# Delta-rule layer: diagonal blocks solved on 128 partitions, moved by copies and 32x32 transposes; the inverses placed earlier in the layer's order

## The chip, the cores and the metric

The kernel runs on one core of a Trainium2 chip. The metric is device time in microseconds (us), the median of several executions. Engines: TensorE (PE, with its weight loads PEld), VectorE (DVE), ScalarE (ACT), GpSimd (POOL), and SyncE (SP), which issues the weight DMAs. Each engine runs its own instructions in the order in which they stand; they wait for each other by semaphores.

## The reference

A decoder trunk of four residual layers over 256 tokens of width 1024: pooling mixer, gated delta rule, latent attention, pooling mixer. The change touches the second. Its core, for each of 8 heads and each chunk of tokens:

```python
L = jnp.where(strict, jnp.einsum('bhnid,bhnjd->bhnij', k_beta, k) * decay, 0.0)
A = jnp.eye(C, dtype=L.dtype) + L
rhs = jnp.concatenate([v_beta, k_beta * jnp.exp(g)[..., None]], axis=-1)
sol = lax.linalg.triangular_solve(A, rhs, left_side=True, lower=True)
...
def step(state, xs):
    q_c, k_c, u_c, w_c, g_c, a_c = xs
    v_new = u_c - jnp.einsum('bhck,bhkv->bhcv', w_c, state)
    o = (jnp.einsum('bhck,bhkv->bhcv', q_c * jnp.exp(g_c)[..., None], state)
         + jnp.einsum('bhij,bhjv->bhiv', a_c, v_new))
    ...
```

So a unit lower triangular matrix I + L has to be inverted for each head and chunk.

## The kernel before, in words

Every large product goes through `project`: 512 columns of a weight matrix are loaded by SP in units of two slices of 128 rows (`weights`, L133), each slice is split into a high part on ACT (L149, `whi`) and a low part on DVE, for a few slices on POOL (L150, `wlo`), and PE accumulates three products of split operands (L162). The raw loads have three buffers, the split slices a ring of them, so PE can lag behind the splits. A projection "by channels" (`chan`) has matmuls of 256 columns, one by rows has 512.

The delta-rule layer (`gdn_layer`) takes two tiles of 128 tokens (`NT` = 2) and eight heads, in place of chunks of 64. The string `order` fixes the sequence in which its parts are written: `g` gates, `k` keys (projection, convolution on DVE L750, SiLU on ACT L787, transposes L793), `d` decays, `a` the lower triangles `LT` (L806 on PE, L813 on DVE), `s` the substitution, `q` queries, `v` values (a value's convolution L750, SiLU L902, transposes L906, scaling into `vR` L909), `V` and `c` the two halves of the last value, `i` the inverses, `u` the new values of the first tile. A scheduler then interleaves the written instructions on each engine; its result is fixed when the program is built.

The substitution inverts the 32x32 diagonal blocks of I + L, 64 of them (2 tiles x 8 heads x 4 blocks). Eight DMAs gather them from `LT` into DRAM (`d_l`, L838) and one loads them as `Lb`, one block on each of 64 partitions (L841). Then POOL runs 31 steps of a multiply (L846, into `pr`) and a subtraction (L850, in `Tb`). Step r updates the n = 31 - r rows below row r in c = r + 1 columns, n x c elements on each partition. `Tb` goes back through DRAM (`d_t`, L853, L857) into the diagonal blocks of `T`.

The inverses transpose `T` into `U` by 32x32 blocks on DVE (L929), join blocks in pairs (L938, L940, L944, L947) and then whole (L952, L953, L956, L959, L962, L965), tile after tile; the instructions of PE alternate with DVE or ACT in each. `U` is needed by the new values (L979) and by the recurrence that ends the layer, which begins with L1006 on PE.

Tiles named by `big` share one pool of buffers: a new tile waits until the last reader of its buffer's former tile is done. Before the change the second `kqT` of the queries has the buffer of `Lb`.

Of the kernel before, what the change touches and what calls it, by code (L numbers as in the profile page):

```python
# [8 lines left out]
F32 = mybir.dt.float32  # L9
# [7 lines left out]
P = 128  # L17
D = 1024
S = 256
NT = S // P  # L20
# [22 lines left out]
def trunk(ctx: ExitStack, tc: tile.TileContext, x, positions, norm_g, pool_w_in, pool_w_grp,  # L43
          pool_scale, pool_w_out, gdn_w_in, gdn_conv, gdn_a_log, gdn_dt_bias, gdn_norm_g,
          gdn_w_out, mla_w_in, mla_q_norm_g, mla_w_uq, mla_kv_norm_g, mla_w_ukv, mla_w_out,
          final_g, out, depth=4, final=True):
    nc = tc.nc
# [4 lines left out]
    const = ctx.enter_context(tc.tile_pool(name="const", bufs=1))  # L52
# [11 lines left out]
    dram = ctx.enter_context(tc.tile_pool(name="dram", bufs=1, space=bass.MemoryType.DRAM))  # L64


    def big(name, *dims, dt=F32):
        return s4.tile([P, *dims], dt, tag="s4", name=name)
# [4 lines left out]
    def workb(name, *dims):  # L73
        return wb.tile([P, *dims], F32, tag="wb", name=name)

    def small(name, *dims, bufs=2):
        return sm.tile([P, *dims], F32, tag=name, name=name, bufs=bufs)

    def bank(pool, name):
        return pool.tile([P, CW], F32, tag=name, name=name)  # L80
# [29 lines left out]
    def inorder(a, n=P):  # L110

        if len(a.shape) == 3 and a.shape[2] != n:
            a = a.rearrange("p h s -> p (h s)")
        if len(a.shape) == 3:
            return a.rearrange("p h (a b) -> p h a b", b=2)
        return a.rearrange("p (g a b) -> p g a b", a=n // 2, b=2)

    def woven(a, n=P):

        if len(a.shape) == 3 and a.shape[2] != n:  # L120
            a = a.rearrange("p h s -> p (h s)")
        if len(a.shape) == 3:
            return a.rearrange("p h (b a) -> p h a b", b=2)
        return a.rearrange("p (g b a) -> p g a b", a=n // 2, b=2)
# [191 lines left out]
    half = const.tile([P, 1], F32, name="half")  # L316
# [291 lines left out]
    GC = {}  # L608

    def gdn_setup():  # L610
        w_in = gdn_w_in[0]
        utri = const.tile([P, P], F32, name="utri")
        nc.gpsimd.memset(utri, 1.0)
        nc.gpsimd.affine_select(out=utri, in_=utri, compare_op=ALU.is_ge, fill=0.0, base=0,
                                pattern=[[1, P]], channel_multiplier=-1)
        maskT = const.tile([P, P], F32, name="maskT")
        nc.gpsimd.memset(maskT, 0.0)
        nc.gpsimd.affine_select(out=maskT, in_=maskT, compare_op=ALU.is_ge, fill=NEG, base=0,
                                pattern=[[1, 2], [2, P // 2]], channel_multiplier=-1)
        m32 = const.tile([P, 2, 32], F32, name="m32")  # L620
        nc.gpsimd.memset(m32, 0.0)
        for a in range(2):
            nc.gpsimd.memset(m32[64 * a + 32:64 * a + 64, a], 1.0)
        half = const.tile([P, NT, GDN_H // 2], F32, name="halves")
        nc.gpsimd.memset(half, -0.5)


        crow = workb("crow", P)
        nc.scalar.dma_start(out=crow, in_=gdn_conv[0].rearrange("k (n p) -> (k n) p", p=P))
        tap = const.tile([P, P], F32, name="tap")  # L630
        ps = bank(tps, "tp")
        nc.tensor.transpose(ps[:, :P], crow, ident)
        nc.vector.tensor_copy(tap, ps[:, :P])

        bw = workb("bw", KD, 16)
        bws = const.tile([P, KD, 2, 16], F32R, name="bws")
        nc.scalar.dma_start(out=bw, in_=w_in[:, 2 * GDN_QK + 2 * GDN_V:].rearrange(
            "(k p) c -> p k c", p=P))
        nc.vector.tensor_copy(bws[:, :, 0, :], bw)
        nc.vector.tensor_tensor(out=bws[:, :, 1, :], in0=bw, in1=bws.bitcast(F32)[:, :, 0, :],  # L640
                                op=ALU.subtract)
        alog = const.tile([P, GDN_H], F32, name="alog")
        nc.scalar.dma_start(out=alog, in_=gdn_a_log[0:1, :].to_broadcast([P, GDN_H]))
        dtb = const.tile([P, GDN_H], F32, name="dtb")
        nc.scalar.dma_start(out=dtb, in_=gdn_dt_bias[0:1, :].to_broadcast([P, GDN_H]))
        GC.update(utri=utri, maskT=maskT, m32=m32, half=half, tap=tap, bws=bws,
                  alog=alog, dtb=dtb)

    def gdn_layer(i, j, hT):
        H = GDN_H  # L650
        M = NT * H
        DV = 256
        w_in = gdn_w_in[j]
        utri, maskT, m32, half, tap, bws, alog, dtb = (
            GC[n] for n in ("utri", "maskT", "m32", "half", "tap", "bws", "alog", "dtb"))

        def sc(name):
            return small(name, NT, H, bufs=1)
# [11 lines left out]
                gated = nc.scalar.activation(*unpaired(gs[vi][:, t, :], banks[t]), AF.Silu)  # L670
            mark["gate"] = gated.ins

        order = "g0 k0 d a0 g1 k1 a1 s q0 v0 v1 v2 q1 V3 i c3 g2 u0 u1 g3".split()
        while order[0][0] == "g":
            gate(int(order.pop(0)[1]))

# [9 lines left out]
        for t in range(NT):  # L686
# [8 lines left out]
                                in1=dtb[:, None, :].to_broadcast([P, NT, H]))  # L695
# [13 lines left out]
                                in1=alog[:, None, :].to_broadcast([P, NT, H]))  # L709
# [14 lines left out]
        for t in range(NT):  # L724
            nc.gpsimd.dma_start(
                out=Gb[t].rearrange("p h s -> p (h s)"),
                in_=d_g[t * H:(t + 1) * H, :].rearrange("(a h) s -> a (h s)", a=1).to_broadcast(
                    [P, H * P]))
# [24 lines left out]


        Q, B = 4, 32
        Tb = big("Tb", B, B)[:M * Q]
        nc.gpsimd.memset(Tb, 0.0)
        nc.gpsimd.memset(Tb.rearrange("m r c -> m (r c)")[:, ::B + 1], 1.0)
        Ts = big("T", NT, H, P)
        T = [Ts[:, t] for t in range(NT)]  # L760
        for t in range(NT):
# [39 lines left out]
        def against(dst, rhs, sf, hf, t):  # L801

            ps = bank(aux, "aux").rearrange("p (b s) -> p b s", b=4)
            tt = slice(t * P, (t + 1) * P)
            for b in range(4):
                nc.tensor.matmul(ps[:, b], lhsT=kT[hf][:, b, tt], rhs=rhs[hf][:, b, tt],  # L806
                                 start=True, stop=True)
            for b in range(4):
                h = 4 * hf + b
                o, v, d = dst[t][:, h, :], ps[:, b], DT[t][:, h, :]  # L810
                if dst is LT:
                    o, v, d = inorder(o), inorder(v), woven(d)
                nc.vector.scalar_tensor_tensor(  # L813
                    out=o, in0=v, scalar=sf[:, t, h:h + 1], in1=d, op0=ALU.mult, op1=ALU.mult)

        LT = [big("LT", H, P) for _ in range(NT)]
# [11 lines left out]
        def lower(hf):  # L828
            for t in range(NT):
                against(LT, kT, s2, hf, t)  # L830

        def substitution():

            d_l = dram.tile([M * Q, B * B], F32, name="d_l")
            lv = d_l.rearrange("(t m d) (r c) -> t d r m c", t=NT, d=Q, r=B)
            for t in range(NT):
                for d in range(Q):
                    nc.sync.dma_start(out=lv[t, d],  # L838
                                      in_=LT[t][d * B:(d + 1) * B, :, d * B:(d + 1) * B])
            Lb = big("Lb", B, B)[:M * Q]  # L840
            nc.sync.dma_start(out=Lb, in_=d_l.rearrange("m (r c) -> m r c", r=B))  # L841
            pr = small("pr", 256, bufs=1)[:M * Q]
            for r in range(B - 1):
                n, c = B - 1 - r, r + 1
                pv = pr[:, :n * c].rearrange("m (a b) -> m a b", a=n)
                nc.gpsimd.tensor_tensor(out=pv, op=ALU.mult,  # L846
                                        in0=Lb[:, r, r + 1:, None].to_broadcast([M * Q, n, c]),
                                        in1=Tb[:, r:r + 1, :c].to_broadcast([M * Q, n, c]))
                tv = Tb[:, r + 1:, :c]
                mark["blocks"] = nc.gpsimd.tensor_tensor(out=tv, in0=tv, in1=pv,  # L850
                                                         op=ALU.subtract).ins
            d_t = dram.tile([M * Q, B * B], F32, name="d_t")
            nc.gpsimd.dma_start(out=d_t.rearrange("m (r c) -> m r c", r=B), in_=Tb)  # L853
            tv = d_t.rearrange("(m d) (r c) -> d r m c", d=Q, r=B)
            for d in range(Q):
                dd = slice(d * B, (d + 1) * B)
                nc.gpsimd.dma_start(out=Ts[dd, :, :, dd].rearrange("p t h c -> p (t h) c"),  # L857
                                    in_=tv[d])
            nc.vector.reciprocal(rki, rk)
            nc.vector.tensor_tensor(out=kds, in0=rk[:, 0, :], in1=DT[0][:, :, P - 1],  # L860
                                    op=ALU.mult)
            nc.vector.tensor_scalar(neG, eG[:, 1, :], -1.0, None, ALU.mult)
            nc.gpsimd.tensor_tensor(out=ktok, in0=ktok, op=ALU.mult,
                                    in1=kds[:, :, None].to_broadcast([P, H, P]))
# [52 lines left out]
        u1 = []  # L917
# [84 lines left out]
        st, vn, v2 = {}, {}, {}  # L1002
# [408 lines left out]
```

## Time and profile before

| | before |
|---|---|
| median of 3 runs | 829.0 us (827.01 to 829.16) |
| profiled execution: time, span | 832.1 us, 830.4 us |
| granted TensorE clock, mean | 0.986 |
| busy, share of the span: PE, DVE, ACT, POOL | 96%, 73%, 59%, 19% |
| delta-rule layer, first gate to the recurrence's first product | about 175 to 355 us |

PE's matmuls overlap in a pipeline, so its busy share alone doesn't tell whether it waits; the slices, the granted clock and the list of waits do. In rows of waits the numbers are the total, the count and the longest. In rows of instructions, start and duration come first; in brackets is how long the engine was idle before and what ended that. The lines themselves stand in the prediction.

### The profile page before, as it was taken

The numbers are of one execution on the slowest core, as the hardware profiler recorded it, in microseconds if no ns is written. First come the engines' busy times: TensorE is split into PE (matmuls) and PEld (weight loads), VectorE is DVE, ScalarE is ACT, GpSimd is POOL, SyncE is SP. The second block draws the span as 40 slices with busy tenths as digits, with TensorE's granted clock in tenths as the row PEclk, the third lists the DMA queues.
The fourth block names the chain that finished last, engine by engine and source line by source line (L and its number), as shares of the span: only waits on it lengthen the run. The fifth ranks groups of instructions, "written<-read, shape, count | busy, mean of one in ns | idle before, by whom it ended". The sixth has DMA issues, their size and how long they took to land.

```text
span 830.4 us, 16162 instructions
## 1 busy us (share of the span) xinstructions
PE 799.4 (96%) x5966; PEld 758.0 (91%) x5966; DVE 603.4 (73%) x1141; ACT 492.9 (59%) x993; POOL 159.8 (19%) x296
## 2 busy tenths in 40 slices
PE   8989999999898979999999999999999999999996
PEld 7989988989898978788989999999999989999996
DVE  4699887666987967356666678778877767877772
ACT  6665565567855655255566564666665565566662
POOL 2001100334236992023121112000000120000012
PEclk9999999999999989899999999999999999999998
DMA  6865666756655544303647786653552547576662
GB/s 204 224 180 167 193 209 210 221 153 195 193 135 180 163 139 118 124 12 115 187 125 224 231 180 185 192 164 102 153 175 80 179 143 214 183 223 202 202 204 51
DMA packets 109079, 139.90 MB, mean 168 GB/s; under 512 B 21316, under 2 KB 51208, under 8 KB 109000
## 3 DMA queue, kind: packets, MB, share of 16 engines
q1 hardware_dynamic: 106608, 137.12, 55.0%
q0 software_dynamic: 528, 1.58, 0.6%
q8 instruction: 47, 0.77, 0.4%
q10 hardware_dynamic: 1864, 0.17, 0.2%
q14 instruction: 32, 0.26, 0.1%
HBM read 137.27 MB, written 1.58 MB: 167 GB/s over the span
## 4 chain that ended last, share of the span: by engine, by line
PE 67%; DVE 11%; POOL 8%; DMA 8%; issue 4%; ACT 2%; SPq 0%; POOLq 0%; DVEq 0%; ACTq 0%
PE acc L162 53%; PE aux L162 7%; POOL pr L846 3%; DVE wlo L154 3%; POOL Tb L850 2%; DMA raw<-in_pool_w_out_dram 2%; DVE wlo L150 1%; DMA raw<-in_pool_w_in_dram 1%; DVE win L551 1%; DMA T<-d_t 1%; DMA Lb<-d_l 1%; DVE h L397 1%; DMA Gb<-d_g 1%; PE aux L979 1%; PE tp L1314 1%
## 5 line engine op out<-in xcount | busy, mean ns | idle before, releaser
L150 DVE TENSOR_TENSOR wlo<-raw,whi 128x512 fp32r<-128x512 f32 (+1 forms) x366 | 254.2, 719 | 104.3 <-ACT whi L149 100.8
L149 ACT CAST whi<-raw 128x512 fp32r<-128x512 f32 (+1 forms) x380 | 223.7, 617 | 167.6 <-PE acc L162 82.3
L162 PE MATMUL acc<-hTh,whi 128*128 128x256 f32 x832 | 230.7, 278 | 2.3 <-ACT gsg L670 1.5
L162 PE MATMUL acc<-hTl,whi 128*128 128x256 f32 x832 | 231.2, 278 | 0.0
L162 PE MATMUL acc<-hTh,wlo 128*128 128x256 f32 x832 | 229.8, 277 | 0.0
L162 PEld LDWEIGHTS acc<-hTh,whi 128*128 128x128 f32 x832 | 160.7, 193 | 2.9 <-ACT gsg L670 1.7
L162 PEld LDWEIGHTS acc<-hTl,whi 128*128 128x128 f32 x832 | 160.8, 193 | 0.3
L162 PEld LDWEIGHTS acc<-hTh,wlo 128*128 128x128 f32 x832 | 160.7, 193 | 0.1
L162 PE MATMUL acc<-wlo,yTh 128*128 128x256 f32 (+1 forms) x384 | 112.7, 312 | 0.8 <-DVE wlo L154 0.8
L162 PE MATMUL acc<-whi,yTh 128*128 128x256 f32 (+1 forms) x384 | 112.3, 315 | 0.0
L162 PE MATMUL acc<-whi,yTl 128*128 128x256 f32 (+1 forms) x384 | 89.1, 313 | 0.0
L162 PEld LDWEIGHTS acc<-wlo,yTh 128*128 128x128 f32 x384 | 73.2, 191 | 4.8 <-DVE wlo L154 1.7
L162 PEld LDWEIGHTS acc<-whi,yTh 128*128 128x128 f32 x384 | 72.9, 191 | 3.1
L162 PEld LDWEIGHTS acc<-whi,yTl 128*128 128x128 f32 x384 | 63.1, 191 | 3.4
L154 DVE SCALAR_TENSOR_TENSOR wlo<-raw,colsT,whi 128x512 fp32r<-128x512 f32 x64 | 47.0, 769 | 21.1 <-ACT whi L153 20.7
L153 ACT ACTIVATE whi<-raw,gain 128x512 fp32r<-128x512 f32 x64 | 43.6, 720 | 31.1 <-DMA raw<-in_pool_w_in_dram 22.6
L153 ACT ACTIVATE whi<-raw,colsT 128x512 fp32r<-128x512 f32 x64 | 43.5, 720 | 30.9 <-DMA raw<-in_pool_w_out_dram 18.0
L385 POOL TENSOR_TENSOR hg<-x,gain 128x256 f32<-128x256 f32 x16 | 13.4, 850 | 244.1 <-DVE x L450 244.1
L162 PE MATMUL acc<-wlo,hTh 128*128 128x512 f32 (+1 forms) x144 | 54.8, 385 | 1.9 <-DVE wlo L150 1.3
L154 DVE SCALAR_TENSOR_TENSOR wlo<-raw,gain,whi 128x512 fp32r<-128x512 f32 x64 | 46.6, 748 | 11.1 <-ACT whi L153 11.1
L162 PE MATMUL acc<-whi,hTh 128*128 128x512 f32 (+1 forms) x144 | 52.7, 379 | 0.7 <-ACT hTh L242 0.7
L162 PE MATMUL acc<-whi,hTl 128*128 128x512 f32 (+1 forms) x144 | 42.5, 373 | 0.0
(364 smaller groups left out, 1530.9 us busy)
## 6 DMA issues: line engine op xcount, KB each, us to landing
raw<-in_pool_w_in_dram SPq DMA_DIRECT2D x62, 512.0 KB, 4.4
raw<-in_gdn_w_in_dram SPq DMA_DIRECT2D x48, 512.0 KB, 4.0
raw<-in_pool_w_out_dram SPq DMA_DIRECT2D x32, 512.0 KB, 4.4
raw<-in_mla_w_in_dram SPq DMA_DIRECT2D x24, 512.0 KB, 4.5
raw<-in_mla_w_uq_dram SPq DMA_DIRECT2D x36, 256.0 KB, 3.4
raw<-in_pool_w_grp_dram SPq DMA_DIRECT2D x16, 512.0 KB, 3.8
raw<-in_gdn_w_out_dram SPq DMA_DIRECT2D x16, 512.0 KB, 3.8
raw<-in_mla_w_ukv_dram SPq DMA_DIRECT2D x32, 256.0 KB, 3.3
```

The source lines that it names most:

```text
L149: a = nc.scalar.copy(hi, v)
L150: b = e.tensor_tensor(out=lo, in0=v, in1=hi.bitcast(F32), op=ALU.subtract)
L153: a = nc.scalar.activation(hi, v, AF.Copy, scale=g)
L154: b = e.scalar_tensor_tensor(out=lo, in0=v, scalar=g, in1=hi.bitcast(F32), op0=ALU.mult, op1=ALU.subtract)
L162: return nc.tensor.matmul(inorder(o, n), lhsT=lhs, rhs=woven(rhs, n), start=start, stop=stop)
L385: nc.gpsimd.tensor_tensor(out=self.early[t, a], in0=xs[t][:, sl], in1=self.g[:, sl], op=ALU.mult)
L397: nc.vector.scalar_tensor_tensor(out=h[:, cut:], in0=xs[t][:, sl], scalar=r[:, 0:1], in1=self.g[:, sl], op0=ALU.mult, op1=ALU.mult)
L551: nc.vector.tensor_tensor(out=nxt[:, :, d:], in0=cur[:, :, d:], in1=cur[:, :, :S - d], op=ALU.add)
L846: nc.gpsimd.tensor_tensor(out=pv, op=ALU.mult, in0=Lb[:, r, r + 1:, None].to_broadcast([M * Q, n, c]), in1=Tb[:, r:r + 1, :c].to_broadcast ...
L850: mark["blocks"] = nc.gpsimd.tensor_tensor(out=tv, in0=tv, in1=pv, op=ALU.subtract).ins
L979: nc.tensor.matmul(ps[:, c], lhsT=U[0][:, h, :], rhs=vR[h // 2][:, 0, c * DV:(c + 1) * DV], start=True, stop=True)
L1314: nc.tensor.transpose(ps[:, a * P:(a + 1) * P], sb[:, a * P:(a + 1) * P], ident)
```

## The change

The 64 blocks are spread over all 128 partitions: partition p of a 32-partition band holds for one of the 16 tile-and-head pairs either the even or the odd columns of the block, 16 of 32. Each step then has c = r // 2 + 1 columns. The blocks reach `Lb` by copies into `Lg` (tile 0 on POOL, tile 1 on ACT) and one DVE transpose of 32x32 blocks that reads each block twice; the result goes back by a second such transpose into the other half of `solve` and four copies into `T`, two on POOL and two on ACT. All DMAs of this part fall away. `which`, built in layer 0, marks the even and the odd half and gives the unit diagonal. In `order` the inverses `i` move from behind `V3` to behind `v1`.

```diff
+        cols = workb("cols", 2, 32)
+        for a in range(2):
+            nc.gpsimd.memset(cols[:, a, :16], 1.0 - a)
+            nc.gpsimd.memset(cols[:, a, 16:], float(a))
+        which = const.tile([P, 2, 32], F32, name="which")
+        nc.vector.transpose(which.rearrange("p a c -> p (a c)"), cols.rearrange("p a c -> p (a c)"))
...
-        order = "g0 k0 d a0 g1 k1 a1 s q0 v0 v1 v2 q1 V3 i c3 g2 u0 u1 g3".split()
+        order = "g0 k0 d a0 g1 k1 a1 s q0 v0 v1 i v2 q1 V3 c3 g2 u0 u1 g3".split()
...
-        Tb = big("Tb", B, B)[:M * Q]
+        C = B // 2
+        solve = big("solve", 2, B, C)
+        Tb, turned_ = solve[:, 0], solve[:, 1]
         nc.gpsimd.memset(Tb, 0.0)
-        nc.gpsimd.memset(Tb.rearrange("m r c -> m (r c)")[:, ::B + 1], 1.0)
+        for a in range(2):
+            nc.gpsimd.tensor_copy(Tb.rearrange("p r c -> p (r c)")[:, a * C::B + 1],
+                                  which[:, a, :C])
+        Lg = small("Lg", M, B, bufs=1)
...
         def lower(hf):
             for t in range(NT):
                 against(LT, kT, s2, hf, t)
+                hs = slice(4 * hf, 4 * hf + 4)
+                for d in range(Q):
+                    dd = slice(d * B, (d + 1) * B)
+                    o = Lg[dd, t * H + 4 * hf:t * H + 4 * hf + 4]
+                    if t:
+                        nc.scalar.copy(o, LT[t][dd, hs, dd])
+                    else:
+                        nc.gpsimd.tensor_copy(o, LT[t][dd, hs, dd])
...
-            d_l = dram.tile([M * Q, B * B], F32, name="d_l")
-            lv = d_l.rearrange("(t m d) (r c) -> t d r m c", t=NT, d=Q, r=B)
-            for t in range(NT):
-                for d in range(Q):
-                    nc.sync.dma_start(out=lv[t, d],
-                                      in_=LT[t][d * B:(d + 1) * B, :, d * B:(d + 1) * B])
-            Lb = big("Lb", B, B)[:M * Q]
-            nc.sync.dma_start(out=Lb, in_=d_l.rearrange("m (r c) -> m r c", r=B))
-            pr = small("pr", 256, bufs=1)[:M * Q]
+            Lb = big("Lb", B, B)
+            nc.vector.transpose(Lb, Lg.rearrange("p m c -> p c m")[:, :, None, :].to_broadcast(
+                [P, B, 2, M]))
+            pr = small("pr", 136, bufs=1)
             for r in range(B - 1):
-                n, c = B - 1 - r, r + 1
+                n, c = B - 1 - r, r // 2 + 1
                 pv = pr[:, :n * c].rearrange("m (a b) -> m a b", a=n)
                 nc.gpsimd.tensor_tensor(out=pv, op=ALU.mult,
-                                        in0=Lb[:, r, r + 1:, None].to_broadcast([M * Q, n, c]),
-                                        in1=Tb[:, r:r + 1, :c].to_broadcast([M * Q, n, c]))
+                                        in0=Lb[:, r + 1:, r:r + 1].to_broadcast([P, n, c]),
+                                        in1=Tb[:, r:r + 1, :c].to_broadcast([P, n, c]))
...
-            d_t = dram.tile([M * Q, B * B], F32, name="d_t")
-            nc.gpsimd.dma_start(out=d_t.rearrange("m (r c) -> m r c", r=B), in_=Tb)
-            tv = d_t.rearrange("(m d) (r c) -> d r m c", d=Q, r=B)
+            nc.vector.transpose(turned_.rearrange("p r c -> p (r c)"),
+                                Tb.rearrange("p r c -> p c r"))
+            tv = turned_.rearrange("p r c -> p (r c)").rearrange("p (c m) -> p m c", m=M)
             for d in range(Q):
                 dd = slice(d * B, (d + 1) * B)
-                nc.gpsimd.dma_start(out=Ts[dd, :, :, dd].rearrange("p t h c -> p (t h) c"),
-                                    in_=tv[d])
+                o = Ts[dd, :, :, dd].rearrange("p t h c -> p (t h) c")
+                if d % 2:
+                    nc.scalar.copy(o, tv[dd])
+                else:
+                    nc.gpsimd.tensor_copy(o, tv[dd])
```

The change adds lines ahead of most of the layer, so line numbers move: L750 becomes L756, L793 L804, L806 L817, L906 L923, L909 L926, L929 L946, L979 L996, L1006 L1023. Outside this layer the engines' orders are the same but for the setup's five small instructions and one matmul of layer 0.

DVE, in the stretch in which v2 is convolved (`vc`) while the next weight slices are split. Before:

```order
L750 SCALAR_TENSOR_TENSOR vc<-acc,tap,vc 128x254
L750 SCALAR_TENSOR_TENSOR vc<-acc,tap,vc 128x253
L750 SCALAR_TENSOR_TENSOR vc<-acc,tap,vc 128x255
L150 TENSOR_TENSOR wlo<-raw,whi 128x512
L750 SCALAR_TENSOR_TENSOR vc<-acc,tap,vc 128x253
L750 SCALAR_TENSOR_TENSOR vc<-acc,tap,vc 128x255
L150 TENSOR_TENSOR wlo<-raw,whi 128x512
L750 SCALAR_TENSOR_TENSOR vc<-acc,tap,vc 128x254 x2
L150 TENSOR_TENSOR wlo<-raw,whi 128x512
L750 SCALAR_TENSOR_TENSOR vc<-acc,tap,vc 128x253 x2
L150 TENSOR_TENSOR wlo<-raw,whi 128x512 x3
```

And now:

```order
L756 SCALAR_TENSOR_TENSOR vc<-acc,tap,vc 128x255
L866 STREAM_TRANSPOSE solve<-solve 128x512
L150 TENSOR_TENSOR wlo<-raw,whi 128x512
L756 SCALAR_TENSOR_TENSOR vc<-acc,tap,vc 128x253
L756 SCALAR_TENSOR_TENSOR vc<-acc,tap,vc 128x255
L150 TENSOR_TENSOR wlo<-raw,whi 128x512
L756 SCALAR_TENSOR_TENSOR vc<-acc,tap,vc 128x254 x2
L756 SCALAR_TENSOR_TENSOR vc<-acc,tap,vc 128x253
L150 TENSOR_TENSOR wlo<-raw,whi 128x512
L756 SCALAR_TENSOR_TENSOR vc<-acc,tap,vc 128x253
L150 TENSOR_TENSOR wlo<-raw,whi 128x512 x2
L946 STREAM_TRANSPOSE U<-T 128x1024 x2
```

The transpose of the solved blocks (L866) now stands in the middle of v2's convolution, and the transposes into `U` directly behind it; before, they stood behind the second queries.

ACT, where v1 is scaled into `vR`. Before:

```order
L902 ACTIVATE vc<-vc 128x512
L149 CAST whi<-raw 128x512 x2
L909 ACTIVATE vR<-tp,rki 128x256 x4
L149 CAST whi<-raw 128x512 x3
L902 ACTIVATE vc<-vc 128x512 x2
```

And now:

```order
L919 ACTIVATE vc<-vc 128x512
L149 CAST whi<-raw 128x512 x2
L926 ACTIVATE vR<-tp,rki 128x256 x2
L873 COPY T<-solve 32x16x32 x2
L926 ACTIVATE vR<-tp,rki 128x256 x2
L149 CAST whi<-raw 128x512 x3
L919 ACTIVATE vc<-vc 128x512 x2
```

Two of the copies into `T` stand between the scalings; this `vR` now has the buffer of `Lb`, and the second `kqT` of the queries has one of its own.

PE, at the end of the inverses and the start of the recurrence. Before, the second tile's last steps follow each other:

```order
L162 MATMUL acc<-whi,hTl_2253 128x512 x2
L962 MATMUL aux<-U,X 64x64 x8
L952 MATMUL aux<-ident,U 64x64 x8
L956 MATMUL aux<-T,LT 128x64 x8
L962 MATMUL aux<-U,X 64x64 x8
L979 MATMUL aux<-vR,U 128x256 x8
L1006 MATMUL aux<-u_4405,ktok 128x256 x2
```

And now the first of the new values come behind the last step of the second tile, with accumulations of the last gate (`hTh`, `hTl` are the layer's input) between them:

```order
L162 MATMUL acc<-whi,hTh_2250 128x512
L979 MATMUL aux<-U,X 64x64 x8
L817 MATMUL aux<-kqT 128x128 x8
L996 MATMUL aux<-vR,U 128x256 x2
L162 MATMUL acc<-wlo,hTh_2250 128x512
L162 MATMUL acc<-whi,hTl_2251 128x512 x2
L162 MATMUL acc<-whi,hTh_2250 128x512
L162 MATMUL acc<-wlo,hTh_2250 128x512
L162 MATMUL acc<-whi,hTh_2250 128x512
```

In all, 30 accumulations stand between the last L996 and the recurrence's L1023, where there were none; ahead of the last L979 stand 17 behind its L973, 22 and 26 between the steps before.

More of the change, by code (lines that the diff above doesn't have):

```diff
@@ L645, in gdn_setup @@
         nc.scalar.dma_start(out=dtb, in_=gdn_dt_bias[0:1, :].to_broadcast([P, GDN_H]))
-        GC.update(utri=utri, maskT=maskT, m32=m32, half=half, tap=tap, bws=bws,
+        GC.update(utri=utri, maskT=maskT, m32=m32, half=half, which=which, tap=tap, bws=bws,
                   alog=alog, dtb=dtb)
@@ L653, in gdn_layer @@
         w_in = gdn_w_in[j]
-        utri, maskT, m32, half, tap, bws, alog, dtb = (
-            GC[n] for n in ("utri", "maskT", "m32", "half", "tap", "bws", "alog", "dtb"))
+        utri, maskT, m32, half, which, tap, bws, alog, dtb = (
+            GC[n] for n in ("utri", "maskT", "m32", "half", "which", "tap", "bws", "alog", "dtb"))
         def sc(name):
```

## The prediction

> **What bounds the kernel now.** I read the chain of work that ended last first, then the busy time and the granted TensorE clock in slices of 4 us, then who waits for whom, then the instructions of the engines named there.
>
> ```profile
> PE 67%; DVE 11%; POOL 8%; DMA 8%; issue 4%; ACT 2%; SPq 0%; POOLq 0%; DVEq 0%; ACTq 0%
> ```
>
> Two thirds of the chain are matmuls, so an edit pays only where TensorE (PE) stands still or runs at a lower clock. POOL, busy for 19% of the span, holds 8% of the chain: nearly all of it is the substitution (L846, L850) between 255 and 301 us, with the DMAs ahead of it and behind it. The slices below carry window, length, then for PE, PEld, DVE, ACT and POOL busy us and instructions, then clock, DMA share, GB/s.
>
> ```profile
> 268.00:272.00 4.00, 2.02 (x17) 1.83 (x16) 4.00 (x9) 2.39 (x4) 3.69 (x5) 0.96 0.53 139
> 272.00:276.00 4.00, 4.00 (x25) 4.00 (x24) 4.00 (x9) 3.27 (x8) 3.61 (x6) 0.62 0.66 203
> ...
> 296.00:300.00 4.00, 0.14 (x2) 0.00 (x0) 1.11 (x3) 0.00 (x0) 3.38 (x9) 0.87 0.43 136
> 300.00:304.00 4.00, 3.17 (x15) 3.17 (x16) 2.68 (x5) 3.22 (x7) 3.70 (x8) 0.50 0.07 16
> 304.00:308.00 4.00, 4.00 (x30) 4.00 (x30) 2.33 (x4) 1.40 (x3) 4.00 (x5) 0.78 0.32 53
> ...
> 344.00:348.00 4.00, 2.55 (x23) 2.27 (x21) 1.79 (x3) 0.58 (x1) 0.00 (x0) 0.84 0.38 133
> 348.00:352.00 4.00, 4.00 (x21) 3.43 (x20) 0.68 (x1) 0.41 (x2) 0.00 (x0) 0.50 0.01 4
> 352.00:356.00 4.00, 4.00 (x15) 3.07 (x14) 0.33 (x1) 2.84 (x8) 0.00 (x0) 0.80 0.00 0
> ```
>
> Three holes show, each followed by slices at a lower clock. What PE waited for in them (us in total, times, longest):
>
> ```profile
> PE tp L793 <- ACT kqT L787: 4.7, 1, 4.7
> PE tp L906 <- ACT vc L902: 2.5, 2, 2.0
> PE acc L162 <- DVE vc L750: 0.8, 1, 0.8
> PE aux L962 <- DVE X L959: 0.8, 1, 0.8
> PE aux L956 <- ACT T L953: 0.7, 1, 0.7
> ...
> ACT kqT L787 <- POOL pr L846: 5.5, 1, 5.5
> ```
>
> **Hole A**, 269 us: the transposes of v0 wait 2.0 us for its convolution on VectorE (DVE), which is busy for all of the slices 268 to 276. The lower clock costs 0.04x4 + 0.38x4 = 1.7 us: 3.7 us together.
> **Hole B**, 296 us: ScalarE (ACT) can't write the second q until POOL's last multiply, because that kqT gets the buffer of Lb. PE loses 4.7 us, and 0.50x4 + 0.22x4 = 2.9 us of clock behind it: 7.6 us.
> **Hole C**, 344 to 356 us: the last steps of the inverses stand alone on PE and wait for DVE and ACT (0.8 + 0.7 us); clock 0.16x4 + 0.50x4 + 0.20x4 = 3.4 us: 4.9 us.
> Beside these stands a wait of 0.8 us for v2's convolution at 288 us, where V3 needs an accumulator.
>
> **The substitution, shorter and sooner.**
>
> ```profile
> L846 POOL TENSOR_TENSOR pr<-Lb,Tb 64x31 f32<-64x31 f32 (+15 forms) x31 | 21.3, 686 | 16.9 <-DMA Lb<-d_l 14.5
> L850 POOL TENSOR_TENSOR Tb<-Tb,pr 64x31 f32<-64x31 f32 (+15 forms) x31 | 19.2, 620 | 2.4
> L150 DVE TENSOR_TENSOR wlo<-raw,whi 128x512 fp32r<-128x512 f32 x24 | 21.3, 898 | 2.9 <-ACT whi L149 2.9
> ...
> 255.39 0.23 POOL L846 TENSOR_TENSOR pr<-Lb,Tb 64x31 f32<-64x31 f32 x1 [14.55 <-DMA Lb<-d_l]
> 255.70 0.26 POOL L850 TENSOR_TENSOR Tb<-Tb,pr 64x31 f32<-64x31 f32 x1
> ...
> 275.86 0.62 POOL L846 TENSOR_TENSOR pr<-Lb,Tb 64x255 f32<-64x255 f32 x1
> ```
>
> It runs from 255.4 to 300.6 us: 45.2, of which 40.5 busy and 4.7 gaps. The rows of 31 and 255 elements give (0.62 - 0.23)/224 = 1.74 ns an element and 0.18 us fixed. So 62 x 0.18 = 11.2 us are fixed, and the multiplies' and subtractions' 5,456 elements each (the sum of n x c in the loop) take about 20.1; the rest, some 9 us, is blocking: the DVE subtraction of two SBUF operands, L150, takes 898 ns in the mean here and 0.69 us alone (the row at 257.11 below), and 9/24 = 0.37 us of POOL's time goes to each of the 24. In the change c is r//2 + 1, which sums to 2,856 elements, 52%. That gives 11.2 + 4.7 + 0.52 x 20.1 + 18 blockings of 0.37 (18 such DVE instructions now stand beside it) = 33 us. The bounds: 26 us without any blocking, and 45 us, as long as now, should an instruction on 128 partitions cost twice what it does on 64. I take 33: POOL's multiply of 128x512 below takes 1.27 us, which fits 0.18 + 512 x 1.74 = 1.07 and some blocking, and not twice that.
>
> Its start: LT is done at 242.82 + 1.89 = 244.7 us, and Lb is there 10.6 us later, through eight DMAs and one back.
>
> ```profile
> 242.82 1.89 DVE L813 SCALAR_TENSOR_TENSOR LT<-aux,s,DT 128x128 f32<-128x128 f32 x7
> 243.70 3.79 SPq L838 DMA_DIRECT2D d_l<-LT  x8
> 249.16 0.45 SPq L841 DMA_DIRECT2D Lb<-d_l  x1
> ...
> 256.46 0.62 ACT L149 CAST whi<-raw 128x512 fp32r<-128x512 f32 x1 [2.92 <-DMA raw<-in_gdn_w_in_dram]
> 257.11 0.69 DVE L150 TENSOR_TENSOR wlo<-raw,whi 128x512 fp32r<-128x512 f32 x1 [2.85 <-ACT whi L149]
> ...
> 314.95 2.37 DVE L929 STREAM_TRANSPOSE U<-T 128x1024 f32<-128x1024 f32 x2 [3.06 <-DMA T<-d_t]
> ```
>
> Now four copies on POOL and four on ACT take that place, side by side, 128 elements each: between 0.23 us (31 elements on POOL) and 0.62 (255 on POOL, 512 on ACT); I take 0.3, nearer to the first, and both engines are done at 246. The DVE transpose of 128x1024 takes 2.37/2 = 1.2 us and stands behind queued work, near 248. The solve starts at 249.5 and ends at 282.5 us.
>
> SP's nine issues go as well, with the weight loads held behind them: DVE's idle 2.85 us at 254 (a whi that waited 2.92 us for its load) goes, and DVE runs 2.9 us ahead through the convolutions. That closes hole A: **-3.7 us**. The new 1.2 us transpose falls into the other idle time of DVE in this stretch.
>
> **What now waits for the solve.** DVE's transpose of the result (L866) stands between the convolutions of v2, ACT's copies into T (L873) and v1's vR, which now gets Lb's buffer, between the scalings of v1.
>
> ```profile
> 283.47 1.25 DVE L750 SCALAR_TENSOR_TENSOR vc<-acc,tap,vc 128x254 f32<-128x254 f32 x3
> 284.64 0.68 DVE L150 TENSOR_TENSOR wlo<-raw,whi 128x512 fp32r<-128x512 f32 x1
> ...
> 300.60 1.27 POOL L878 TENSOR_TENSOR Gb<-Gb,kqT 128x512 f32<-128x512 f32 x1
> 303.48 1.85 POOL L772 TENSOR_TENSOR rq<-rq,halves 128x8 f32<-128x8 f32 x1
> ```
>
> L866 stands between these two DVE rows, at 284.6 less 2.9 and less some blocking: near 281. So DVE and ACT wait some 1.5 us for the solve's end at 282.5; behind DVE are queued weight subtractions and the rest of v2's convolution, which V3's accumulator waits for. Half of an 128x1024 transpose is 0.6 us, then the 4.8 us of queue that stand there now: v2 is done at 288. PE, 3.7 us earlier by hole A, is there at 288.3 - 3.7 = 284.6 and waits 3.5 us in place of 0.8: **+2.7**. A wait of that size cost 1.7 us of clock in hole A: **+1.7**.
> T: POOL first does L895 and a power (1.27 and 1.85 us as above) with two small instructions, then its two copies of 512 elements (0.62 to 1.27 each, I take 0.8): T is whole near 289, DVE's U transposes are due at 291, and PE gets to the first pairs at 289 to 290. DVE is the later one, so this costs little.
> Hole B goes, since no buffer of q waits for Lb any more: **-7.6**. Hole C goes: by the order the last steps of both tiles now have 15 to 30 accumulations between them, as only the first tile's had before:
>
> ```profile
> 332.62 4.95 PE acc L162 x22
> ```
>
> Twenty-two of them cover 4.95 us, and DVE and ACT answer in one: **-4.9**. In their place I count 1.5 us of short waits (PE for the masked X behind the U transposes, and for an accumulator under the second q's scores): **+1.5**. ACT's first four copies of LT stand ahead of the second keys' convolution: 4 x 0.3 = **+1.2**; the other four stand ahead of weight casts, which are prefetched, and cost nothing unless that lead is used up (then 1.2 more). The setup's four memsets and one small transpose lie beside layer 0's matmuls, at nothing; without that cover they cost five short instructions, 5 x 0.23 = 1.2 us.
>
> **Sum**: -3.7 + 2.7 + 1.7 - 7.6 - 4.9 + 1.5 + 1.2 = **-9.1 us**. Against the profiled execution's 832.1 us (830.4 of span and 1.7 around it) that is 823.0. The median of the runs is 829.0, 3.1 below that execution, so I predict 829.0 - 9.1 = **819.9 us**.
>
> [...] The two first POOL rows have 31 elements each, but the second reads and writes a column of Tb, 128 bytes from element to element: 0.26 against 0.23 us, 1 ns an element. The new multiply reads a column of Lb in the same way. [...]
>
> **Rivals.**
> 1. Column reads lengthen the solve: 2,856 x 1 ns = 2.9 us by the rows above, passed on whole through L866: -9.1 + 2.9 = -6.2, 822.8 us. For it: the pair of rows. Against: rows of longer runs show no such difference, and runs grow to 16. Chance 0.17.
> 2. The tail keeps its waits: in-order DVE and ACT put X, U and T behind convolutions and weight work, and hole C moves rather than goes: -9.1 + 4.9 = -4.2, 824.8 us. Chance 0.13.
> 3. The solve ends before DVE gets to L866 (blocking nearly gone, 30 us or less): L866's 1.5 us, the clock's 1.7 and the 1.5 of short waits fall away: -9.1 - 4.7 = -13.8, 815.2 us. Chance 0.1.
> 4. The other side: an instruction on 128 partitions costs twice its element time, the solve takes 45 us and ends at 294.7. DVE, ACT and then PE stand still at L866 12.2 us longer, with 1.2 us more of clock (hole B's 2.9 against 1.7): -9.1 + 13.4 = +4.3, 833.3 us. It decides from a solve of some 42 us on. Chance 0.06.
> 5. The change does not free PE: the wait for Lb only passes from q to v1's vR and L866, with a solve near 40 us: -9.1 + 7 = -2.1, 826.9 us. Chance 0.04.
>
> **How the numbers follow.** The forecast has 0.5. A measurement of this kernel can tell about 0.3%, 2.5 us, from no change. Cases 1 to 3 and the forecast are faster by more: 0.9; case 5 is the same, 0.04; case 4 slower, 0.06. The range goes from just under case 3, 814.5, to past case 2, 826; the solve's upper bound, case 4, stays outside with case 5.
>
> **What would show it.** Right: no wait of kqT for POOL; a solve of about 33 us that starts near 249.5; L866 waiting 1 to 3 us; one PE wait of 3 to 4 us near 285; full clock from 340 on; the recurrence's first product (L1006, now L1023) near 346 instead of 355 us. Wrong: a solve over 40 us, a wait of DVE at L866 over 5 us, or PE waits of more than 3 us in all between 290 and 345.

## The result, and the profile after

| | before | after |
|---|---|---|
| median, first comparison (6 runs each) | 829.08 us (827.01 to 830.99) | 823.74 us (819.74 to 824.35) |
| ratio to before | | 0.9928, 95% interval 0.9904 to 0.9952 |
| measured again (11 and 6 runs) | 830.19 us | 825.98 us, ratio 0.9949, 0.9929 to 0.9969 |
| profiled execution: time, span | 832.1 us, 830.4 us | 824.35 us, 822.6 us |

The forecast was 819.9 us, with a range of 814.5 to 826.0. The change is faster, as forecast, but brings 4 to 5 us, not 9. The two profiled executions lie 7.8 us apart. Part of that lies ahead of the edited stretch, as the rows of the first convolution and of the recurrence's first product show (durations in ns, then first and last start):

```profile
L750 DVE SCALAR_TENSOR_TENSOR cv<-acc,tap,cv x48: 460/474/483, 197.5 to 304.2; 128x255 f32<-128x255 f32 x16, 128x254 f32<-128x254 f32 x16, 128x253 f32<-128x253 f32 x16
L1006 PE MATMUL aux<-u,ktok x16: 379/379/382, 355.0 to 372.8; 128*128 128x256 f32 x16
```

Before, the recurrence begins 355.0 - 197.5 = 157.5 us behind the first convolution. After:

```profile
L756 DVE SCALAR_TENSOR_TENSOR cv<-acc,tap,cv x48: 460/472/483, 196.0 to 304.1; 128x255 f32<-128x255 f32 x16, 128x254 f32<-128x254 f32 x16, 128x253 f32<-128x253 f32 x16
L1023 PE MATMUL aux<-u,ktok x16: 379/379/382, 346.6 to 365.0; 128*128 128x256 f32 x16
```

346.6 - 196.0 = 150.6 us, 6.9 less. I call this distance the stretch; it compares profiles without what happens ahead of it. The slices of the changed kernel (window, length, then PE, PEld, DVE, ACT, POOL busy, clock, DMA share, GB/s):

```profile
268.00:272.00 4.00, 4.00 (x37) 4.00 (x38) 4.00 (x9) 3.42 (x9) 3.61 (x6) 1.00 0.61 200
...
280.00:284.00 4.00, 2.62 (x24) 2.42 (x22) 0.00 (x0) 0.21 (x1) 3.14 (x12) 1.00 0.00 0
284.00:288.00 4.00, 0.00 (x0) 0.00 (x0) 3.91 (x8) 3.43 (x6) 3.86 (x6) 0.91 0.00 0
288.00:292.00 4.00, 3.33 (x15) 3.07 (x15) 3.69 (x6) 4.00 (x10) 3.49 (x5) 0.50 0.52 138
292.00:296.00 4.00, 4.00 (x21) 4.00 (x20) 4.00 (x7) 1.61 (x4) 0.00 (x0) 0.50 0.58 145
296.00:300.00 4.00, 4.00 (x32) 4.00 (x32) 3.05 (x7) 2.90 (x7) 0.00 (x0) 0.81 0.33 117
...
340.00:344.00 4.00, 4.00 (x20) 3.52 (x19) 1.29 (x2) 2.08 (x5) 0.00 (x0) 1.00 0.18 62
```

Holes A, B and C are gone (no slice from 300 to 360 us is below full clock), and one new hole stands at 283 us, with a low clock from 287 to 297 us. Who waited for whom there, on PE, DVE and ACT:

```profile
PE acc L162 <- DVE vc L756: 5.9, 1, 5.9
...
DVE solve L866 <- POOL solve L864: 6.6, 1, 6.6
...
ACT vR L926 <- POOL pr L860: 7.0, 1, 7.0
```

PE waits for v2's convolution, which is queued behind L866 on DVE, which waits for the solve. ACT stands for the same time at v1's vR, whose buffer was Lb's. The rows around it (start, duration, idle before):

```profile
249.29 0.61 POOL L860 TENSOR_TENSOR pr<-Lb,solve 128x31 f32<-128x31 f32 x1 [5.03 <-DVE Lb L854]
...
283.83 0.22 POOL L864 TENSOR_TENSOR solve<-solve,pr 128x16 f32<-128x16 f32 x1
...
276.23 1.25 DVE L756 SCALAR_TENSOR_TENSOR vc<-acc,tap,vc 128x254 f32<-128x254 f32 x3
284.09 1.05 DVE L866 STREAM_TRANSPOSE solve<-solve 128x512 f32<-128x512 f32 x1 [6.61 <-POOL solve L864]
...
283.79 0.84 ACT L926 ACTIVATE vR<-tp,rki 128x256 f32<-128x256 f32 x2 [7.02 <-POOL pr L860]
```

The solve takes 34.8 us, from 249.3 to 284.1 (forecast: 33, from 249.5). DVE is at L866 at 277.5 us, not at 281.

### The profile page after: what moved, and what is told of

Read it like the earlier page. It is cut to its first block, busy times and chain, and to the rows that moved or that the text cites. A ratio compares the mean times of both kernels' runs of the same rounds, so it can differ in the third digit from the quotient of the medians.

```text
span 822.6 us, 16161 instructions
## 1 busy us (share of the span) xinstructions
PE 796.2 (97%) x5966; PEld 754.7 (92%) x5966; DVE 601.4 (73%) x1144; ACT 498.1 (61%) x1003; POOL 153.8 (19%) x306
## 4 chain that ended last, share of the span: by engine, by line
PE 73%; DVE 8%; DMA 6%; POOL 6%; issue 4%; ACT 2%; SPq 0%; POOLq 0%; ACTq 0%; DVEq 0%
PE acc L162 58%; PE aux L162 6%; DMA raw<-in_gdn_w_in_dram 2%; POOL solve L864 2%; POOL pr L860 2%; DMA raw<-in_pool_w_in_dram 2%; DVE wlo L150 1%; DVE wlo L154 1%; DVE h L397 1%; DMA Gb<-d_g 1%; DMA raw<-in_pool_w_out_dram 1%; PE tp L1331 1%; ACT whi L149 1%; PE aux L955 1%; DVE win L551 1%
## 5 line engine op out<-in xcount | busy, mean ns | idle before, releaser
L150 DVE TENSOR_TENSOR wlo<-raw,whi 128x512 fp32r<-128x512 f32 (+1 forms) x366 | 248.9, 705 | 99.3 <-ACT whi L149 97.2
L154 DVE SCALAR_TENSOR_TENSOR wlo<-raw,gain,whi 128x512 fp32r<-128x512 f32 x64 | 46.7, 747 | 10.1 <-ACT whi L153 9.9
```

The costliest lines, as they stand in the source:

```text
L150: b = e.tensor_tensor(out=lo, in0=v, in1=hi.bitcast(F32), op=ALU.subtract)
L154: b = e.scalar_tensor_tensor(out=lo, in0=v, scalar=g, in1=hi.bitcast(F32), op0=ALU.mult, op1=ALU.subtract)
```

## The experiments

Lines move a little in kernels with more lines; names tell what they are. Each ratio is to runs of the kernel before on the same chip, whose medians differ by up to 2.6 us from one set to the next. In the table, the stretch is that of each profile, and half clock is how long PE's clock was at 0.50 between 270 and 310 us, worked out from windows of 1 us. Stretch, wait and half clock come from one profile of each run.

| run | median, us | ratio to before (interval) | stretch, us | longest wait of PE, 270 to 300 us | half clock, us |
|---|---|---|---|---|---|
| the change | 823.74 | 0.9928 (0.9904 to 0.9952) | 150.6 | 5.9 | 10.2 |
| change_again | 825.98 | 0.9949 (0.9929 to 0.9969) | 150.8 | 6.2 | 10.2 |
| late | 825.29 | 0.9910 (0.9880 to 0.9940) | 153.2 | 6.0 | 6.8 |
| early_only | 833.69 | 1.0031 (1.0003 to 1.0058) | 160.8 | 3.4 (at 314) | 10.2 (306 to 320) |
| back | 822.46 | 0.9878 (0.9847 to 0.9910) | 148.3 | 5.6 | 6.8 |
| back_lbown | 821.60 | 0.9867 (0.9835 to 0.9898) | 147.2 | 5.6 | 6.8 |
| back_vr | 823.82 | 0.9914 (0.9894 to 0.9934) | 149.7 | 6.3 | 10.2 |
| i_v2 | 825.47 | 0.9948 (0.9928 to 0.9969) | 150.8 | 6.2 | 13.7 |
| back_short | 819.77 | 0.9872 (0.9847 to 0.9897) | 144.9 | 2.8 | 0 |
| copies_first | 819.69 | 0.9875 (0.9848 to 0.9902) | 145.4 | 2.3 | 0 |
| copies_first_again | 819.22 | 0.9871 (0.9847 to 0.9894) | 145.6 | 1.9 | 6.8 |
| pairs_later | 822.00 | 0.9891 (0.9857 to 0.9926) | 147.7 | 3.8 | 10.2 |

### The two halves of the change

late has the new data path and the old place of the inverses:

```diff
-        order = "g0 k0 d a0 g1 k1 a1 s q0 v0 v1 i v2 q1 V3 c3 g2 u0 u1 g3".split()
+        order = "g0 k0 d a0 g1 k1 a1 s q0 v0 v1 v2 q1 V3 i c3 g2 u0 u1 g3".split()
```

> The new data path, with the inverses back at their old place behind V3. Theory: the hole of PE at 283 to 297 us (5.9 us of wait and some 5 us at a lower clock) comes from L866, which keeps its place in the middle of v2's convolution, and from the solve's end, not from the early inverses; so the hole stays, DVE again waits 5 to 7 us at L866, and the tail of the inverses (hole C, 4.9 us) is back: 826 to 830 us, the same as before. Rival (the early inverses put that hole there): the hole goes, hole C is back, 816 to 819 us.

early_only has the old data path through DRAM and the new place:

```diff
-        order = "g0 k0 d a0 g1 k1 a1 s q0 v0 v1 v2 q1 V3 i c3 g2 u0 u1 g3".split()
+        order = "g0 k0 d a0 g1 k1 a1 s q0 v0 v1 i v2 q1 V3 c3 g2 u0 u1 g3".split()
```

> The old data path through DRAM, with the inverses placed behind v1. Theory: holes A and B stay as they are, since they hang on the loads behind SP's issues and on the substitution's end near 300 us; and the inverses, placed sooner, get T no sooner, so the tail stands alone again: 827 to 833 us. Rival (the new place alone spreads the tail): hole C's 4.9 us go, 823 to 825 us.

In late the hole stayed, with L866 again at its place, and the tail stood alone again; the waits of PE and DVE:

```profile
PE acc L162 <- DVE vc L756: 6.0, 1, 6.0
...
PE aux L979 <- DVE X L976: 0.8, 1, 0.8
...
DVE solve L866 <- POOL solve L864: 7.2, 1, 7.2
```

So the hole comes from the solve, not from the inverses' new place. The tail has another 6.8 us of low clock, from 341 to 348 us. The time, 825.3 us, is just under the forecast 826 to 830; but "the same as before" fell, since late is 0.9% faster than the kernel before on its chip. The place alone (early_only) is no gain, and at 833.7 us lies just past its forecast 827 to 833: PE stands at the first pairs until T is back from DRAM.

```profile
PE aux L938 <- DMA T<-d_t: 3.4, 1, 3.4
...
PE aux L962 <- DVE X L959: 0.8, 1, 0.8
```

Hole A stayed here (2.0 us) and is gone in late, so it goes with the path; the weight loads and DVE's shorter subtractions were not tried apart. Hole B did not stay as forecast: no q waits for the solve any more, but PE waits 2.9 us at 303 us for a weight subtraction that POOL does behind it.

By the stretches, the path alone is worth 4.3 us, the place alone -3.3, both 6.9. The ratios don't bear out that the place adds to the path: late's 0.9910 and the change's 0.9928 and 0.9949 have overlapping intervals, and late's is the lowest. The gain that is shown is the path's.

### What waits for the solve

back puts the transpose back and the copies into T into a function of their own, written behind v2, and holds them until v2's last convolution instruction has been issued:

```diff
-        order = "g0 k0 d a0 g1 k1 a1 s q0 v0 v1 i v2 q1 V3 c3 g2 u0 u1 g3".split()
+        order = "g0 k0 d a0 g1 k1 a1 s q0 v0 v1 v2 b i q1 V3 c3 g2 u0 u1 g3".split()
...
+            elif name == "b":
+                with later(mark["conv"]):
+                    back()
```

> The change, with the transpose of the solved blocks (L866, here L874) and the copies into T held behind v2's convolution, and the inverses placed behind that. v1's vR still gets Lb's buffer. Theory: the solve's end is waited for in two places, by DVE and by ACT; with DVE free, ACT still waits some 5 us at vR for the last multiply, the casts behind it stop and PE runs out of slices: part of the hole stays, 817 to 822 us. Rival (only L866 matters): the whole hole of 11 us goes, 811 to 814 us. Second rival (the wait only moves on, to T and U): 823 us or more.

back_lbown gives Lb another tile besides:

```diff
-            Lb = big("Lb", B, B)
+            Lb = small("Lb", B, B, bufs=1)
```

> As the run before, with a buffer of its own for Lb, so that neither DVE nor ACT waits for the solve in the middle of v2. Theory: no wait of PE over 2 us between 270 and 300 us and no lower clock there: 811 to 815 us. Rival (the wait only moves on, to T and U behind them): PE stands still at the first pairs instead, 820 us or more.

In back, DVE no longer waits for the solve itself, but PE waits as long as before, through ACT (rows of PE, DVE and ACT):

```profile
PE acc L162 <- DVE vc L756: 5.6, 1, 5.6
...
DVE wlo L150 <- ACT whi L149: 8.2, 2, 7.4
...
ACT vR L928 <- POOL pr L860: 8.4, 1, 8.4
```

vR stands for 8.4 us, the casts stand behind it, the weight subtractions wait for the casts, and v2's convolution is queued behind these. I had counted on only part of the hole staying; nearly all of its wait stayed (5.6 us of 5.9), with a shorter low clock behind it, and the time, 822.5 us, lies just past the forecast 817 to 822. In back_lbown both forecasts fell: PE stood as long as before, and not at the first pairs, though the time is past the 820 us of the second. v1's vR then got the buffer of the first q instead, which is read by a POOL product queued behind the solve (rows of PE and ACT):

```profile
PE tp L925 <- ACT vc L921: 5.6, 1, 5.6
...
ACT vR L928 <- POOL Gb L897: 8.2, 1, 8.2
```

back_vr is back with a buffer for v1's vR that is taken ahead of the solve:

```diff
+            held_v.append(big("vR", NT, CW))
+            nc.gpsimd.memset(held_v[0][:, 0, :1], 0.0)
...
-            vR.append(big("vR", NT, CW))
+            vR.append(held_v.pop() if vi == 1 else big("vR", NT, CW))
```

> As the run back, and v1's vR now has a buffer of its own, which nothing of the solve or of POOL's later products holds (its first word is written ahead of the solve, so that the buffer can't be shared). Theory: DVE and ACT each waited for the solve alone, in back only ACT; with both free no wait of PE over 2 us stands between 270 and 300 us, the clock stays full there, and the 5.6 us of wait and about 2.4 us of clock that back still had go: 812 to 816 us. Rival (the wait moves on, to the first pairs, since T is whole only some 6 us after the solve): PE stands still for 3 us or more at the pairs, 818 us or more.

The rival was right. No engine waits for the solve in v2 any more, and PE runs to the first pairs and stands there for T. The wait of PE, and then POOL's instructions behind the solve:

```profile
PE aux L961 <- POOL T L887: 6.3, 1, 6.3
```

```profile
286.79 1.28 POOL L901 TENSOR_TENSOR Gb<-Gb,kqT 128x512 f32<-128x512 f32 x1
288.15 0.52 POOL L902 TENSOR_SCALAR rq<-ssq 128x8 f32<-128x8 f32 x1
288.76 1.96 POOL L783 TENSOR_TENSOR rq<-rq,halves 128x8 f32<-128x8 f32 x1
290.80 0.73 POOL L905 TENSOR_TENSOR rq<-rq 128x8 f32<-128x8 f32 x1
291.62 0.25 POOL L906 TENSOR_SCALAR rq<-rq 128x8 f32<-128x8 f32 x1
291.82 2.50 POOL L887 COPY T<-solve 32x512 f32<-32x512 f32 x2
```

Five instructions for the queries, whose results nothing needs before the recurrence, hold the copies from 286.8 to 291.8 us. copies_first puts them behind the copies, and ktok's product too, which in back_vr stood ahead of the solve, at 239 us:

```diff
+                    mark["copied"] = nc.gpsimd.tensor_copy(o, tv[dd]).ins
+            with later(mark["copied"]):
+                nc.gpsimd.tensor_tensor(out=ktok, in0=ktok, op=ALU.mult,
+                                        in1=kds[:, :, None].to_broadcast([P, H, P]))
+                for rest in put_off:
+                    rest()
```

> The run back_vr, with POOL's two copies into T directly behind the solve and the products of ktok and of the first queries behind them. In back_vr these stood ahead and took 5 us, and PE waited 6.3 us at the first pairs for the copies. Theory (the wait is for T and nothing else): T is whole some 3.9 us after the solve, near 290.5, PE waits 2 to 3 us at the pairs and has one or two clock steps behind it: 817 to 821 us. Rival (DVE's U or the masked X is as late): the wait at the pairs or just behind them stays at 5 us or more, 822 us or more.

```profile
PE tp L804 <- ACT kqT L798: 2.3, 1, 2.3
PE aux L970 <- POOL T L885: 1.7, 1, 1.7
```

The wait for T fell to 1.7 us, a second one of 2.3 stands behind it, and the clock stayed full, where I had counted on a step or two of low clock; the time, 819.7 us, is as forecast. It was measured again in the same rounds as the change:

> The change itself once more, on the same chip and in the same rounds as the run copies_first_again, so that the two can be compared. Theory: 0.990 to 0.995 of the time before, as at first. Rival (its gain depended on the chip and the rounds): 0.988 or less, no different from copies_first.

> The run copies_first once more, beside the change. Theory (neither DVE nor ACT waits for the solve in v2, PE waits only 1.7 us for T, and no step of low clock follows): 0.985 to 0.990 of the time before, 3 to 5 us under the change. Rival (the first measurement was only better by its rounds): within 2 us of the change.

819.2 against 826.0 us, and the intervals of the ratios, 0.9847 to 0.9894 and 0.9929 to 0.9969, lie apart: copies_first beats both kernels. The gap to the change, 6.8 us, is larger than the forecast 3 to 5. Its profile was not as forecast: PE waits 1.9 us for T and not for q, and 6.8 us of low clock follow. pairs_later moves the inverses behind the second queries as well (`v2 b q1 i V3`):

> The run copies_first with the inverses one place later, behind the second queries, so that 27 more accumulations and the first transposes of the second q stand ahead of the first pairs. Theory (solve and copies are then covered everywhere): no wait of PE over 2 us between 270 and 300 us, clock full there, and the tail still has accumulations between its steps: 812 to 817 us. Rival (the second q's convolution, queued behind L866 and the U transposes on DVE, is now late): PE waits 3 us or more for kqT, 818 us or more.

The rival was right again: PE does not wait for T, but 3.8 us for the second q, whose convolution DVE has behind L876 and 3.8 us of waiting for the solve. The solve's end is still the wall; it only moves from one reader to the next.

back_short cuts the solve itself (27 of its 31 steps are done):

```diff
-            for r in range(B - 1):
+            for r in range(B - 5):
```

> The run back with the last 4 of the 31 steps of the solve left out (their products are not subtracted); order and buffers are those of back. The left-out steps took 2.6 us in the change. Theory (PE's wait for v2 is as long as the solve, through ACT's vR, the casts behind it and DVE's subtractions): the wait of 5.6 us falls to about 3.0, the clock has the same steps or one of 3.4 us fewer, so 2.6 to 4.3 us less than back: ratio to before 0.983 to 0.985. Rival (the wait comes from v2's convolution or the weights, not from the solve): wait and time as in back, 0.988.

PE's wait for v2 fell from 5.6 to 2.8 us and the clock stayed full: the wait goes with the solve's length. The median fell by 2.7 us against back, but the ratios, 0.9872 and 0.9878, can't be told apart: the forecast 0.983 to 0.985 was missed, and the size of the gain is not shown.

### The clock, and DVE beside POOL

i_v2 has the inverses behind v2 and is otherwise the change (`v0 v1 v2 i q1 V3`):

> The change with the inverses one place later, behind v2; L866 and the copies stand where they stood. Theory on the clock: the same wait of 6 us, but without the products of 32 columns of the first pairs behind it the clock is back at full some 4.7 us after PE resumes, as in late and back, not after 9.0 us as in the change: some 2 us less than the change, 820 to 823 us. Rival (the longer low clock came from the length of the wait): the clock again takes 8 us or more, 823 to 825 us.

The clock was low for 13.7 us, 9.7 of them after PE resumes, and the time, 825.5 us, is past both forecasts. But the run does not test the theory. The new place in `order` did not move the first pairs off the hole: their 16 products, of 64 columns each, stand in the low clock in i_v2 as in the change, where in back they stand behind it. Rows of PE in i_v2, the change and back:

```profile
290.64 0.95 PE L955 MATMUL aux<-T,LT 128*128 128x64 f32 x4
292.25 2.66 PE L955 MATMUL aux<-T,LT 128*128 128x64 f32 x12
```

```profile
291.62 3.51 PE L955 MATMUL aux<-T,LT 128*128 128x64 f32 x16
```

```profile
295.34 1.90 PE L957 MATMUL aux<-T,LT 128*128 128x64 f32 x16
```

The rival's 8 us or more came, but its reason fell, since waits of like length in late and back had 6.8 us of low clock.

halved cuts each POOL instruction of the old substitution in two by rows:

```diff
-                nc.gpsimd.tensor_tensor(out=pv, op=ALU.mult,
-                                        in0=Lb[:, r, r + 1:, None].to_broadcast([M * Q, n, c]),
-                                        in1=Tb[:, r:r + 1, :c].to_broadcast([M * Q, n, c]))
+                cuts = [(0, n)] if n < 2 else [(0, n // 2), (n // 2, n)]
+                for y, z in cuts:
+                    nc.gpsimd.tensor_tensor(
+                        out=pv[:, y:z], op=ALU.mult,
+                        in0=Lb[:, r, r + 1 + y:r + 1 + z, None].to_broadcast([M * Q, z - y, c]),
+                        in1=Tb[:, r:r + 1, :c].to_broadcast([M * Q, z - y, c]))
```

> The kernel before, with each multiply and each subtraction of the substitution cut into two halves by rows: the same elements in 122 instructions in place of 62. Theory (a DVE subtraction of two SBUF operands that comes while a POOL instruction runs waits for the rest of it, so shorter POOL instructions cost DVE less): the mean of L150 beside the solve falls from 0.90 us to 0.75 to 0.82, while the solve grows by some 15 us to about 60. Rival (POOL's share of the time, or the partitions, slow DVE): the mean stays at 0.87 or more. In time 840 to 850 us by both.

DVE's subtractions beside the solve (count, busy, mean ns), first in halved, then in the change:

```profile
L150 DVE TENSOR_TENSOR wlo<-raw,whi 128x512 fp32r<-128x512 f32 x29 | 23.5, 831 | 0.7 <-ACT whi L149 0.7
```

```profile
L150 DVE TENSOR_TENSOR wlo<-raw,whi 128x512 fp32r<-128x512 f32 x20 | 14.1, 716 | 0.0
```

898 ns before, 831 with halved instructions, 716 in the change: the direction is that of the theory, the size only a third of the way, just outside the forecast 0.75 to 0.82 us. The one run took 839.05 us, just under the forecast. A subtraction that ran beside a long POOL instruction, in pairs_later (rows of POOL and DVE):

```profile
291.00 2.28 POOL L887 TENSOR_TENSOR ktok<-ktok,kds 128x1024 f32<-128x1024 f32 x1
...
292.07 1.75 DVE L150 TENSOR_TENSOR wlo<-raw,whi 128x512 fp32r<-128x512 f32 x1
```

It took 1.75 us, where one alone took 0.69 (before, at 257.11 us), and ended 0.54 us behind the end of POOL's product (293.82 against 293.28). That the product held it is an inference from these two rows. Why the change got rid of nearly all of this, and halving of little, stays open.

## Why the prediction was right, and where it was off

- **Hole A goes: right.** The slice 268 to 272 is full at full clock, and late and early_only show that it goes with the data path. A smaller hole at 248 to 256 us, where PE lost 0.08 + 1.11 us before, went as well; I had not counted it (-1.2).
- **The solve: right within 2 us.** Start 249.3, length 34.8, end 284.1 against 249.5, 33 and 282.5. Counted from the first convolution (197.5 us before, 196.0 after), the end is 3.1 us later than forecast. The sum had a slip: 2 x 5,456 elements at 1.74 ns are 19.0 us, not 20.1, which puts the forecast at 33.5. POOL's 62 instructions were busy for 29.9 us where 0.18 us and 1.74 ns an element give 21.1; the other 8.8, put down to blocking as in the forecast, are an estimated 0.44 us for each of the 20 subtractions beside them, against 0.37 forecast for 18. The rows without blocking show no price for 128 partitions or for columns (mean in ns):

```profile
L864 POOL TENSOR_TENSOR solve<-solve,pr 128x96 f32<-128x96 f32 x2 | 0.8, 390 | 0.2
L860 POOL TENSOR_TENSOR pr<-Lb,solve 128x96 f32<-128x96 f32 x2 | 0.7, 354 | 0.2
```

  0.18 + 96 x 0.00174 = 0.35 us, what the multiply on 128 partitions takes, though it reads columns: rivals 1 and 4 fell. This row is a weak test of a price for columns, since the multiply uses each element of a column 4 or 12 times there.
- **The step that failed in size: "and waits 3.5 us in place of 0.8".** PE stood still from 282.6 to 288.5 us, 5.9 us, not from 284.6 to 288, so the term is +5.1, not +2.7. Counted from the first convolution, PE came 0.5 us sooner than forecast and v2 was done 2.0 us later: the solve's end is 3.1 us late, and what stands behind it took 4.4 us (284.1 to 288.5), not 5.5.
- **L866's wait: "some 1.5 us" forecast, 6.6 found.** By the prediction's own signs, over 5 us meant wrong. 1.6 of the difference is the solve's later end, 3.5 is DVE, which reached L866 at 277.5, not 281. This second part did not lengthen PE's wait: v2's end hangs on the solve's end, however long DVE has been there. I had let DVE run 2.9 us ahead "less some blocking". It began v's convolutions 3.8 us sooner (256.59 against 260.39), and from there to L866's place it took 20.9 us where it had taken 24.2: 30 convolution instructions took 13 us in both, but 14 subtractions took 10.1 us where 15 had taken 13.6. I had left DVE's share of the blocking as it was (898 ns a subtraction beside the solve, where the change has 716). The row of 1.75 us in pairs_later agrees that a subtraction can be held beside POOL; by what is not shown.
- **The clock behind it: +1.7 forecast, some +4.5 measured.** From 288.5, when PE resumes, to 297.5 it works at half clock: 9.0 / 2. I had taken hole A's price for a wait of like size; but here the low clock came in three steps of some 3.41 us, and the first pairs stood in them (below).
- **Hole B goes, hole C goes: right.** PE does not wait for the second q, and the clock is full from 297.5 us on. The two were priced 0.4 us too high each, since PE stood still for 0.8 us of the low clock that was counted: 7.2 and 4.5 us. Rivals 2 and 3 fell, and rival 5 came true in part: the wait for Lb did pass from q to vR and L866, at 34.8 us of solve already, and the time lies between the forecast and its 826.9. Short waits: 1.5 forecast; between 250 and 347 us the list of PE's waits has none but the hole's. ACT's copies of LT: +1.2 forecast, no wait of PE found.
- **The sum with what was measured**: -3.7 - 1.2 + 5.1 + 4.5 - 7.2 - 4.5 = -7.0 us, against 6.9 in the stretch. That the time still fell into the range is in part luck: the hole cost 5.2 us more than forecast (2.4 of wait, 2.8 of clock), and 3.9 of these were made good by the small hole and by two costs that did not come. The medians give 5.3 and 4.2; the profiled execution of before lies 3.0 above its median, that of after 0.6, so the profiles show more than the medians do. The forecast took the holes of that slower execution off the median.

## What to carry to other kernels

When a serial stretch gets shorter, its neighbours can get faster too (DVE's subtractions beside the solve took 898 ns before and 716 in the change): work out anew when each engine reaches the place where it waits for the result, with the contention that goes, and not only when the result is there. A new place in the written order is not yet a new place on the engine: look where the scheduler put the instructions (i_v2). When a result is late, list all its readers, and the readers of every buffer that it holds; taking one off its wait leaves the next (L866, then vR, then T, then the second q). Work that nobody needs soon goes behind the copies that somebody does: back_vr and copies_first differ by that alone, and PE's wait for T fell from 6.3 to 1.7 us. Their stretches differ by 4.3 us, of which the clock is a part; their ratios, 0.9914 and 0.9875, have intervals that overlap.

## What the runs showed of the hardware that was not expected

In these profiles PE's clock is low in whole steps of some 3.41 us. The windows of 1 us in which it changes, in the kernel before (PE busy, clock, DMA share, GB/s):

```profile
271.00:272.00 1.00, 1.00 (x9) 0.82 0.38 25
275.00:276.00 1.00, 1.00 (x11) 0.97 0.79 262
298.00:299.00 1.00, 0.00 (x0) 0.98 0.81 231
305.00:306.00 1.00, 1.00 (x7) 0.61 0.01 0
346.00:347.00 1.00, 0.80 (x8) 0.87 0.69 264
353.00:354.00 1.00, 1.00 (x5) 0.72 0.00 0
```

Within a low stretch the windows read 0.50, and outside 1.00; so a mean of 0.82 means that 0.64 us were at full and 0.36 at half clock: the changes come at 271.64, 275.06, 298.96, 305.78, 346.74 and 353.56. The low stretches are 3.4, 6.8 and 6.8 us, and the distances between the changes are 1, 7, 2, 12 and 2 times 3.41. In the change and in i_v2:

```profile
287.00:288.00 1.00, 0.00 (x0) 0.63 0.00 0
297.00:298.00 1.00, 1.00 (x9) 0.75 0.44 170
```

```profile
284.00:285.00 1.00, 0.00 (x0) 0.51 0.00 0
297.00:298.00 1.00, 1.00 (x8) 0.66 0.00 0
```

287.26 to 297.50 is 10.2 us, three steps; 284.02 to 297.68 is 13.7, four. The wait alone doesn't set the number: waits of 5.6 to 6.3 us had two, three or four steps. What stands behind the wait goes with it. In late, back and back_lbown the first pairs came after the low clock, which had two steps; in the change (both times), back_vr, pairs_later and i_v2 they stood in it, and it had three or four. PE was busy for all of the step from 290.85 to 294.26 us in i_v2, for the most part with the pairs' products of 64 columns, and the clock stayed at half; it was busy for all of 289.79 to 293.20 us in back, with wider products, and the clock was full behind it. No run changes that width alone, so the cause is not shown.

One program (copies_first) had no low clock in one profile, with waits of 1.7 and 2.3 us, and two steps in the other, behind a wait of 1.9 us. So a wait of PE of some 2 us had a price that differed between these two profiles, 0 and 3.4 us, and longer waits cost up to some 5 (i_v2: 9.7 us of work at half clock). A difference of that size between two single profiles is no evidence of an edit.
